# Weights of a two-block transformer split by DMAs instead of by the vector engines

## The chip, the cores and the metric

One core of one Trainium2 chip. The metric is device time in microseconds of one execution, the median of the runs. The core has a matrix engine (PE, with its weight loads as PEld), a vector engine (DVE), an activation engine (ACT), a general engine (POOL), and a queue that only issues transfers (SP). 16 DMA engines move data between main memory (HBM) and the on-chip memory (SBUF). Matrix products accumulate in PSUM.

## The reference, cut to what matters

x is 512 rows of 1024. The first block is attention of two kinds (differential, and sparse with compressed, selected and window branches), the second is a short convolution, top-k attention with an indexer, and a gated feed-forward:

```python
x = x + concat([o_diff, o_nsa]) @ w_out                       # first block
h = rms_norm(x, g_mix)                                        # second block
c_b, c_c, c_x, q, k, v, iq, ik, iw, g_a, g_b = split(h @ w_in_2)
y_a = short_conv(c_b, c_c, c_x) @ w_branch_a
y_b = dsa_attention(q, k, v, iq, ik, iw, rel_bias) @ w_branch_b
gates = sigmoid(concat([g_a, g_b]) + b_gate)
x = x + (gates[:, :1024] * y_a + gates[:, 1024:] * y_b) @ w_out_2
h2 = rms_norm(x, g_ffn)
x = x + (silu(h2 @ w_ffn_gate) * (h2 @ w_ffn_up)) @ w_ffn_down
return rms_norm(x, g_final)
```

All of it is float32. PE multiplies in a rounded form of it (float32r), so every operand is split into a high part (rounded) and a low part (what the rounding left), and one product is three matmuls: high by high, high by low, low by high (mm3).

## The kernel before, in words

A *unit* is one piece of a weight matrix, 128 partitions by nk by n. `K.unit` lists the units in the order in which they will be used; `_load` (L190) loads the next one into a tile "raw" on SP's queue, `_split` (L198) makes "whi" by a cast on ACT (L203) and "wlo" by a subtraction raw - whi (L205) on POOL or on DVE (the table POOL by phase: every third unit on POOL, every second, every one, or none), and `take` (L214) hands out the next split unit, splits one unit more and loads two beyond that.

The generators gen_ii, gen_i and gen_tt make the dense products from units, in short steps; the attention code runs such steps between its heads (`K.fill`), so that PE has work while softmax runs on DVE, ACT and POOL. Products of attention that must wait are deferred by planned times (LAG, LAG1 = 12000 ns, LAG2). gen_tt takes all its units at once. The order of the second block is: idx0, idx1, bq0, bq1 (three units each, each from two ranges of columns), conv (12 units), ga (8), ya (4), gb (8), then, when attention is done, yb (4), wo2 (four of gen_ii, four of gen_tt), and 40 units of w_ffn_down (32 of 128 x 2 x 256 and, before and after them, four each; the last four go through gen_tt). The gate and up weights of the feed-forward go another way: class Pair (L1252) loads them on SP and splits sums and differences of them on ACT and DVE; the w_ffn_down units are taken in small steps between its products.

Tiles come from a few tags with a fixed number of buffers. Most units are tag "k4" with 13 buffers, which they share with Pair's tiles, the probabilities (PTa), the gains (gB) and others; the small w_ffn_down units are tag "k2" with 19. A tile waits until a buffer of its tag is free. Each engine executes its instructions in order. The framework sets that order when it builds the program, by priority and by a simulated timeline, so an instruction can stand ahead of its place in the source if its inputs and its buffer are there earlier. A DMA is an instruction in the queue of the engine that issues it, and what stands behind it waits with it.

POOL's other work in the second block: the rows of the relative bias (L509 to L519, with two DMAs), the bias sums "bm" (L1498) and the scaling of softmax "p" (L1527) in attention, the power in the norms (L376, L377), and sums of "mg" (L1194).

Of the kernel before, what the change touches and what calls it, by code (L numbers as in the profile page):

```python
# [9 lines left out]
F32 = mybir.dt.float32  # L10
F32R = mybir.dt.float32r
AF = mybir.ActivationFunctionType
OP = mybir.AluOpType
AX = mybir.AxisListType.X

P = 128
# [17 lines left out]
POOL = {"s": 3, "d": 0, "n": 1, "i": 2, "t": 3, "b": 1, "f": 1}  # L34
# [12 lines left out]
class Kernel:  # L47

    def __init__(self, tc, pool, psum, dram, h):
        self.tc = tc  # L50
        self.nc = tc.nc
        self.pool = pool
        self.psum = psum
        self.dram = dram
        self.h = h
        self.clock = 0.0
        self.pending = []
        self.tails = []
        self.serial = 0
        self.queue = []  # L60
        self.after = None
        self.busy = False
        self.done = set()
        self.units = []
        self.raws = {}
        self.parts = {}
        self.loaded = 0
        self.split = 0
        self.taken = 0
        self.phase = "s"  # L70
        self.credit = 0.0
        self.filling = False
# [7 lines left out]
    def ps(self, shape, dt=F32, name="ps"):  # L80
        return self.psum.tile(shape, dt, name=name, tag="ps", bufs=8)
# [98 lines left out]
    def tick(self):  # L180
        c, self.cost = getattr(self, "cost", 0.0), 0.0
        if self.filling and not self.busy:
            self.credit -= c
        self.spend(c)


    def unit(self, srcs, nk, n, cls="k4", ns=5160.0):
        self.units.append((srcs, nk, n, cls, ns))

    def _load(self):  # L190
        srcs, nk, n, cls, _ = self.units[self.loaded]
        raw = self.t(cls, [P, nk, n], F32, "raw")
        for c0, ap in srcs:
            self.nc.sync.dma_start(raw[:, :, c0:c0 + ap.shape[-1]], ap)
        self.raws[self.loaded] = raw
        self.loaded += 1

    def _split(self):  # L198
        _, nk, n, cls, _ = self.units[self.split]
        raw = self.raws.pop(self.split)  # L200
        hi = self.t(cls, [P, nk, n], F32R, "whi")
        lo = self.t(cls, [P, nk, n], F32R, "wlo")
        self.nc.scalar.copy(hi, raw)  # L203
        every = POOL[self.phase]
        (self.nc.gpsimd if every and self.split % every == 0 else self.nc.vector).tensor_tensor(  # L205
            lo, raw, hi.bitcast(F32), op=OP.subtract)
        self.parts[self.split] = (hi, lo)
        self.split += 1

# [19 lines left out]
def krows(w, k0, nk, c0, n):  # L229
    return w[k0 * P:(k0 + nk) * P, c0:c0 + n].rearrange("(k p) n -> p k n", p=P)  # L230
# [18 lines left out]
def build(tc, pool, psum, dram, h):  # L249
    nc = tc.nc  # L250
    K = Kernel(tc, pool, psum, dram, h)
# [34 lines left out]
    def gen_ii(tag, lhs, w, cols, n, parts, evac, packed=True, wr=None, beside=(), cls="k4", ns=5160.0):  # L286
        for k0, nk in parts:
            srcs, c = [], 0
            for c0, m in cols:
                srcs.append((c, krows(w, (wr or 0) + k0, nk, c0, m)))  # L290
                c += m
            K.unit(srcs, nk, n, cls, ns)
            for piece in beside:
                piece.load()

        per = 2 if packed else 1

        def gen():
            banks = None
            for pi, (k0, nk) in enumerate(parts):  # L300
                wh, wl = K.take()
                if banks is None:
                    banks = [ps([P, per, n], name="acc") for _ in range(NT // per)]
                last = pi == len(parts) - 1
                for tt in range(NT):
                    a, bank = tt % per, banks[tt // per]
                    for k in range(nk):
                        K.mm3(bank[:, a, :], lhs(k0 + k, tt), (wh[:, k, :], wl[:, k, :]),
                              pi == 0 and k == 0 and a == 0, last and k == nk - 1)
                    if last and a == per - 1:  # L310
                        evac(tt - a, per, bank)
                    tick()
                    yield
                for piece in beside:
                    piece.step()
                    yield

        K.dense(tag, gen())
# [218 lines left out]
    def pair_split(src, n):  # L537
        q = t(cls(n), [P, n, 2, 64], F32R, "qs")
        A.copy(q[:, :, 0, :], src)
        V.tensor_sub(q[:, :, 1, :], src, f32(q[:, :, 0, :]))  # L540
        return q

    def dup_split(kn, n):
        kh = t(cls(n), [P, n, 2, 64], F32R, "kh")
        kl = t(cls(n), [P, n, 2, 64], F32R, "kl")
        b = kn[:, :, None, :].to_broadcast([P, n, 2, 64])
        A.copy(kh, b)
        V.tensor_sub(kl, b, f32(kh))
        return kh, kl

    def heads_T(src, n, t0, put, wait, tag):
        def go():
            for a in range(n):
                for eng, dst, srcs in put(a):
                    pt = ps([P, len(srcs), P], F32R, name="pt")
                    for c, s in enumerate(srcs):
                        K.tr(pt[:, c, :], s.rearrange("p l d -> p (l d)"), identR)
                    copy(eng, dst[:, :, (t0 + a) * P:(t0 + a + 1) * P], f32(pt))
            tick()
        defer(wait, go, tag)  # L560
# [538 lines left out]
    for nm in ORDER.split():  # L1099
        nm, _, b = nm.partition(":")  # L1100
# [25 lines left out]
    def i_evac(u):  # L1126
        def evac(tt, n, bank):
            qs = pair_split(bank[:, 0, 0:256].rearrange("p (c d) -> p c d", d=64), 4)
            heads_T(None, 1, tt, lambda a: [(A, S["iQ%d" % u], [qs[:, c] for c in range(4)])], LAG["i"], "idx")
            if u == 0:  # L1130
                kh, kl = dup_split(bank[:, :, 256:320], 1)
                heads_T(None, 1, tt, lambda a: [(V, S["iK"], [kh[:, 0], kl[:, 0]])], LAG["i"], "idx")
            else:
                A.activation(iws[:, tt, :], bank[:, 0, 256:264], AF.Copy, scale=8 ** -0.5 * 64 ** -0.5)
        return evac
# [66 lines left out]
        return f  # L1202

    K.after = None
    gen_ii("idx0", h2l, w_in2, [(2176, 256), (2688, 64)], 320, thirds, i_evac(0), packed=False)
    gen_ii("idx1", h2l, w_in2, [(2432, 256), (2752, 8)], 264, thirds, i_evac(1), packed=False)
    gen_ii("bq0", h2l, w_in2, [(1536, 256), (2048, 64)], 320, thirds, bq_evac(0), packed=False)
# [27 lines left out]
    for f0, nf in chunks:  # L1235
# [3 lines left out]
        if f0 + nf < 22:  # L1239
            for c0 in range(0, D, 256):  # L1240
                gen_ii("dn%d_%d" % (f0, c0), lhs, wd, [(c0, 256)], 256, parts_of(nf, 2), add_X(c0), wr=f0,
                       cls="k2", ns=DNS)
# [335 lines left out]
def emit(tc, h, stage="all"):  # L1578
    with tc.tile_pool(name="sb", bufs=1) as pool, \
            tc.tile_pool(name="ps", bufs=1, space=bass.MemoryType.PSUM) as psum, \  # L1580
            tc.tile_pool(name="dr", bufs=1, space=bass.MemoryType.DRAM) as dram, \
            contextlib.nullcontext():
        build(tc, pool, psum, dram, h)
# [18 lines left out]
```

## Time and profile before

| | |
|---|---|
| runs | 1082.15, 1079.30, 1080.58 us; median 1080.58 |
| profiled execution | 1079.54 us, span 1077.8 us |
| granted clock of TensorE, mean | 0.987 |
| PE, PEld busy | 97%, 90% |
| DVE, ACT, POOL busy | 64%, 52%, 38% |
| HBM read, written | 100.50 MB, 6.84 MB |
| DMAs on SP's queue (q1), on POOL's (q0) | 103.21 MB, 2.65 MB |

Times are microseconds from the start of the span. Busy shares are over the span; a matmul's end is modelled. The time of an execution is a little longer than the span of its core. L205 means line 205 of the kernel before.

### The profile page before, as it was taken

How to read it: one execution, taken by the hardware profiler on the slowest of the kernel's cores; microseconds unless marked ns; L12 is line 12 of the kernel's file. 1: busy time of each engine (PE TensorE's matmuls, PEld its weight loads, DVE VectorE, ACT ScalarE, POOL GpSimd, SP SyncE). 2: the span in 40 equal slices, each digit the busy share in tenths (PEclk: the TensorE clock that was granted, in tenths of full speed). 3: DMA queues.
4: the chain of work that ended last, by engine and by line, in shares of the span. 5: the costliest groups of instructions: out<-in, count | busy, mean ns of one | idle time of the engine just before them, and what ended most of it. 6: DMA issues, size and time to landing. Idle time of an engine off the chain costs nothing. (4 is left out here: it accounts for less than half of the span.)

```text
span 1077.8 us, 18966 instructions
## 1 busy us (share of the span) xinstructions
PE 1049.9 (97%) x7254; PEld 971.9 (90%) x7254; DVE 693.2 (64%) x1464; ACT 560.1 (52%) x1156; POOL 409.2 (38%) x403
## 2 busy tenths in 40 slices
PE   7999999999899999999999999988999999999997
PEld 7899898899789999888888888878999999999995
DVE  5777467356984638999125646477986666567734
ACT  5466687657973445523325765254543444444433
POOL 4442376555465241202127976500111222122241
PEclk8999999999999999999999999988999999999999
DMA  6446321321214335333241334421433223333022
GB/s 195 130 111 171 65 60 40 98 60 43 77 40 147 119 93 184 94 95 108 85 117 40 89 117 150 154 78 54 142 109 99 64 75 117 117 118 118 32 88 78
DMA packets 125045, 107.06 MB, mean 99 GB/s; under 512 B 20305, under 2 KB 115986, under 8 KB 124954
## 3 DMA queue, kind: packets, MB, share of 16 engines
q1 hardware_dynamic: 123882, 103.21, 31.5%
q0 software_dynamic: 1072, 2.65, 0.6%
q8 instruction: 57, 0.93, 0.4%
q14 instruction: 34, 0.28, 0.1%
HBM read 100.50 MB, written 6.84 MB: 100 GB/s over the span
## 5 line engine op out<-in xcount | busy, mean ns | idle before, releaser
L205 POOL TENSOR_TENSOR wlo<-raw,whi 128x1024 fp32r<-128x1024 f32 (+4 forms) x100 | 218.6, 2190 | 442.3 <-ACT whi L203 340.6
L163 PE MATMUL acc<-hA,wh 128*128 128x256 f32 x1232 | 223.7, 282 | 0.0
L163 PE MATMUL acc<-hT,whi 128*128 128x512 f32 x608 | 192.1, 395 | 0.2 <-ACT whi L203 0.2
L203 ACT CAST whi<-raw 128x1024 fp32r<-128x1024 f32 (+4 forms) x143 | 132.1, 925 | 115.7 <-PE acc L163 74.7
L163 PEld LDWEIGHTS acc<-hA,wh 128*128 128x128 f32 x1232 | 190.5, 190 | 0.1
L163 PE MATMUL acc<-whi,hT 128*128 128x256 f32 (+3 forms) x896 | 180.8, 291 | 0.5 <-ACT whi L203 0.5
L163 PE MATMUL acc<-hA,wl 128*128 128x256 f32 x616 | 173.1, 281 | 0.2 <-DVE wl L1249 0.2
L163 PEld LDWEIGHTS acc<-whi,hT 128*128 128x128 f32 x896 | 145.3, 191 | 1.3 <-ACT whi L203 0.7
L163 PEld LDWEIGHTS acc<-hT,whi 128*128 128x128 f32 x608 | 112.2, 188 | 23.5 <-ACT whi L203 0.4
L163 PE MATMUL acc<-whi,act 128*128 128x256 f32 (+1 forms) x640 | 132.8, 292 | 0.0
L163 PE MATMUL acc<-wlo,hT 128*128 128x256 f32 (+3 forms) x448 | 129.8, 290 | 0.7 <-POOL wlo L205 0.7
L163 PE MATMUL acc<-hT,wlo 128*128 128x512 f32 x304 | 120.5, 396 | 0.0
L163 PEld LDWEIGHTS acc<-hA,wl 128*128 128x128 f32 x616 | 116.7, 190 | 0.5 <-DVE wl L1249 0.4
L163 PEld LDWEIGHTS acc<-whi,act 128*128 128x128 f32 x640 | 105.0, 188 | 2.9
L1249 DVE TENSOR_TENSOR wl<-raw,wh 128x1024 fp32r<-128x1024 f32 x55 | 67.8, 1235 | 45.7 <-PE acc L163 24.9
L163 PE MATMUL acc<-wlo,act 128*128 128x256 f32 (+1 forms) x320 | 93.7, 293 | 0.0
L1248 ACT CAST wh<-raw 128x1024 fp32r<-128x1024 f32 x55 | 57.9, 1052 | 60.1 <-PE acc L163 41.8
L617 ACT ACTIVATE p<-p,s 128x128 f32<-128x128 f32 (+3 forms) x128 | 72.1, 565 | 31.5 <-DVE s L615 28.3
L163 PEld LDWEIGHTS acc<-wlo,hT 128*128 128x128 f32 x448 | 85.2, 190 | 1.4 <-POOL wlo L205 1.0
L205 DVE TENSOR_TENSOR wlo<-raw,whi 128x1024 fp32r<-128x1024 f32 (+5 forms) x43 | 52.8, 1231 | 41.1 <-ACT whi L203 41.0
L163 PEld LDWEIGHTS acc<-hT,wlo 128*128 128x128 f32 x304 | 57.2, 188 | 11.6
L163 PEld LDWEIGHTS acc<-wlo,act 128*128 128x128 f32 x320 | 60.2, 188 | 1.4
(271 smaller groups left out, 2011.7 us busy)
## 6 DMA issues: line engine op xcount, KB each, us to landing
raw<-in_w_in SPq DMA_DIRECT2D x52, 512.0 KB, 3.6
raw<-in_w_ffn_gate SPq DMA_DIRECT2D x22, 512.0 KB, 4.9
raw<-in_w_ffn_up SPq DMA_DIRECT2D x22, 512.0 KB, 6.1
raw<-in_w_ffn_down SPq DMA_DIRECT2D x36, 256.0 KB, 6.3
raw<-in_w_out SPq DMA_DIRECT2D x16, 512.0 KB, 3.6
raw<-in_cmp_w SPq DMA_DIRECT2D x8, 512.0 KB, 3.4
raw<-in_w_in SPq DMA_DIRECT2D x10, 384.0 KB, 3.7
rel_all<-rel_rows POOLq DMA_DIRECT2D x1, 2560.0 KB, 17.2
```

The lines of the kernel that those rows point to most:

```text
L163: self.nc.tensor.matmul(out, lhsT, rhs, start=start, stop=stop, skip_group_check=True)
L203: self.nc.scalar.copy(hi, raw)
L205: (self.nc.gpsimd if every and self.split % every == 0 else self.nc.vector).tensor_tensor(lo, raw, hi.bitcast(F32), op=OP.subtract)
L617: S["exp"] = A.activation(p[:, :n], p[:, :n], AF.Exp, scale=-1.0, bias=nm, accum_out=z).ins
L1248: A.copy(hi, src)
L1249: eng.tensor_tensor(lo, src, f32(hi), op=OP.subtract)
```

## The change: who splits a weight unit

For units that are listed after `K.by_dma = True`, that is all units of the second block, the raw tile is gone. The load goes to the queue of POOL and writes float32r, so the DMA rounds and the loaded tile is the high part. ACT writes the negative of the high part into the low part's tile. A second DMA on POOL's queue then loads the same weights from HBM again and adds them to what stands in that tile, which leaves weight minus high part.

```diff
     def unit(self, srcs, nk, n, cls="k4", ns=5160.0):
-        self.units.append((srcs, nk, n, cls, ns))
+        self.units.append((srcs, nk, n, cls, ns, self.by_dma))
 
     def _load(self):
-        srcs, nk, n, cls, _ = self.units[self.loaded]
-        raw = self.t(cls, [P, nk, n], F32, "raw")
+        srcs, nk, n, cls, _, by_dma = self.units[self.loaded]
+        raw = self.t(cls, [P, nk, n], F32R if by_dma else F32, "whi" if by_dma else "raw")
         for c0, ap in srcs:
-            self.nc.sync.dma_start(raw[:, :, c0:c0 + ap.shape[-1]], ap)
+
+            (self.nc.gpsimd if by_dma else self.nc.sync).dma_start(raw[:, :, c0:c0 + ap.shape[-1]], ap)
...
     def _split(self):
-        _, nk, n, cls, _ = self.units[self.split]
+        srcs, nk, n, cls, _, by_dma = self.units[self.split]
         raw = self.raws.pop(self.split)
-        hi = self.t(cls, [P, nk, n], F32R, "whi")
-        lo = self.t(cls, [P, nk, n], F32R, "wlo")
-        self.nc.scalar.copy(hi, raw)
-        every = POOL[self.phase]
-        (self.nc.gpsimd if every and self.split % every == 0 else self.nc.vector).tensor_tensor(
-            lo, raw, hi.bitcast(F32), op=OP.subtract)
+        if by_dma:
+
+            hi, lo = raw, self.t(cls, [P, nk, n], F32R, "wlo")
+            self.nc.scalar.activation(lo, hi.bitcast(F32), AF.Copy, scale=-1.0)
+            for c0, ap in srcs:
+                self.nc.gpsimd.dma_start(lo[:, :, c0:c0 + ap.shape[-1]], ap, accum_op=OP.add)
+        else:
+            hi = self.t(cls, [P, nk, n], F32R, "whi")
+            lo = self.t(cls, [P, nk, n], F32R, "wlo")
+            self.nc.scalar.copy(hi, raw)
+            every = POOL[self.phase]
+            (self.nc.gpsimd if every and self.split % every == 0 else self.nc.vector).tensor_tensor(
+                lo, raw, hi.bitcast(F32), op=OP.subtract)
...
     K.after = None
+    K.by_dma = True
     gen_ii("idx0", h2l, w_in2, [(2176, 256), (2688, 64)], 320, thirds, i_evac(0), packed=False)
```

## Rows read from the trace of the kernel before

**Rows 1.** Busy time, share of the span and instructions, from the page.

```profile
PE 1049.9 (97%) x7254; PEld 971.9 (90%) x7254; DVE 693.2 (64%) x1464; ACT 560.1 (52%) x1156; POOL 409.2 (38%) x403
```

**Rows 2.** Chain of waits, a piece: start us, us, engine, line.

```profile
748.39 322.30 PE acc L163 x2638
```

**Rows 3.** What PE waited for: us in total, times, longest us.

```profile
PE pt L177 <- DVE xs L1360: 7.2, 2, 3.7
PE acc L163 <- POOL wlo L205: 0.7, 1, 0.7
```

**Rows 4.** Busy us by stage, granted clock, DMA share, GB/s.

```profile
360.00:434.00 74.00, 73.93 (x534) 72.09 (x533) 47.84 (x100) 38.02 (x82) 22.54 (x44) 1.00 0.45 134
434.00:567.00 133.00, 133.00 (x592) 109.26 (x592) 87.24 (x169) 44.79 (x61) 26.69 (x13) 1.00 0.34 99
567.00:640.00 73.00, 73.00 (x398) 62.46 (x397) 42.50 (x152) 49.30 (x135) 59.45 (x68) 1.00 0.24 73
640.00:700.00 60.00, 59.31 (x357) 52.33 (x356) 31.48 (x36) 25.62 (x41) 38.27 (x23) 1.00 0.48 158
700.00:760.00 60.00, 51.72 (x359) 49.13 (x358) 48.49 (x60) 31.61 (x48) 3.29 (x5) 0.89 0.23 75
760.00:1078.00 318.00, 310.68 (x2542) 305.97 (x2540) 204.34 (x227) 135.27 (x189) 74.37 (x47) 0.99 0.29 95
```

**Rows 5.** Groups by line, 376 to 1078 us: count, busy us, mean ns, idle before.

```profile
L205 POOL TENSOR_TENSOR wlo<-raw,whi 128x512 fp32r<-128x512 f32 (+3 forms) x71 | 148.7, 2099 | 409.9 <-ACT whi L203 318.9 <-DVE gu L1312 50.6 <-PE acc L163 37.8
L203 ACT CAST whi<-raw 128x1024 fp32r<-128x1024 f32 (+4 forms) x91 | 79.1, 870 | 94.8 <-PE acc L163 65.9 <-issue 12.9 <-POOL wlo L205 6.6
```

**Rows 6.** The same of 360 to 434 us, then of 567 to 640 us.

```profile
L205 POOL TENSOR_TENSOR wlo<-raw,whi 128x960 fp32r<-128x960 f32 (+4 forms) x7 | 14.6, 2092 | 43.8 <-ACT whi L203 37.0 <-PE acc L163 6.8
L205 POOL TENSOR_TENSOR wlo<-raw,whi 128x1024 fp32r<-128x1024 f32 x8 | 19.5, 2448 | 6.3 <-ACT whi L203 6.2
```

**Rows 7.** DMA view, 434 to 567 us: bytes; issues, KB each, us to landing.

```profile
DMA packets 22653, 13.12 MB, mean 99 GB/s; under 512 B 432, under 2 KB 22261, under 8 KB 22645
raw<-in_w_in SPq DMA_DIRECT2D x19, 512.0 KB, 3.6
```

**Rows 8.** Timeline, conv's casts and first matmuls: start us, us, what.

```profile
417.35 1.07 ACT L203 CAST whi<-raw 128x1024 fp32r<-128x1024 f32 x1
433.11 0.65 PE L163 MATMUL acc<-hT,whi 128*128 128x512 f32 x2
451.96 1.05 ACT L203 CAST whi<-raw 128x1024 fp32r<-128x1024 f32 x1 [2.70 <-PE acc L163]
468.48 1.06 ACT L203 CAST whi<-raw 128x1024 fp32r<-128x1024 f32 x1 [3.10 <-PE acc L163]
```

**Rows 9.** Timeline of POOL, 398 to 404 us: its two DMAs.

```profile
399.86 0.82 POOL L518 DMA_DIRECT2D rel_rows<-rel  x1
402.30 1.12 POOL L519 DMA_DIRECT2D rel_all<-rel_rows  x1 [1.61 <-DMA rel_rows<-rel]
```

**Rows 10.** DMA view: the same two, KB each, us from issue to landing.

```profile
rel_all<-rel_rows POOLq DMA_DIRECT2D x1, 2560.0 KB, 17.2
rel_rows<-rel POOLq DMA_DIRECT2D x1, 20.0 KB, 2.1
```

**Rows 11.** Busy us of the stage before the feed-forward, as rows 4.

```profile
638.00:688.00 50.00, 49.31 (x317) 44.37 (x316) 26.76 (x29) 23.76 (x33) 38.53 (x19) 1.00 0.50 163
```

**Rows 12.** Timelines of SP, POOL and PE around the last units of wo2.

```profile
672.75 4.11 SPq L194 DMA_DIRECT2D raw<-in_w_out  x2
675.64 11.64 POOL L205 TENSOR_TENSOR wlo<-raw,whi 128x1024 fp32r<-128x1024 f32 x5
685.61 0.40 PE L163 MATMUL acc<-wlo,mg 128*128 128x512 f32 x1
```

**Rows 13.** Timelines of SP and PE where the feed-forward begins.

```profile
708.79 0.92 SPq L1265 DMA_DIRECT2D raw<-in_w_ffn_gate  x2
716.21 1.12 PE L177 MATMUL pt<-identF,xs 128*128 128x128 f32 x4 [3.53 <-DVE xs L1360]
```

More of the change, by code (lines that the diff above doesn't have):

```diff
@@ L67, in __init__ @@
         self.loaded = 0
+        self.by_dma = False
         self.split = 0
```

## The prediction

> **What bounds the kernel now.** I read the busy shares first: PE is busy 97% of the span, DVE 64%, ACT 52%, POOL 38% [rows 1]. A busy PE can still be held up between its pieces, so the chain of waits comes next: its last long piece is one unbroken run of 2638 matmuls, 322.30 us [rows 2]. Then PE's waits: over the whole span PE waited 0.7 us for a low part (wlo) of a weight; its one large wait is 7.2 us in two pieces for DVE's xs, which are activations, not weights [rows 3]. Last the stages. From 360 us on, which is where second-block weights are split, PE idles 16.4 us of 718 (718 - 701.63, the sum of the stages' PE column): nearly all of it in 700 to 760 us (8.28 us, at a mean clock of 0.89) and at the end of the program (7.32 us) [rows 4]. So PE's own work bounds the kernel, and splits are hidden already. An edit that makes splitting cheaper has that 0.7 us to win directly; an edit that makes a split arrive late loses time at full price.
>
> **The change, part by part.** 96 second-block units (12 of idx and bq, 12 conv, 8 ga, 4 ya, 8 gb, 4 yb, 8 wo2, 40 of w_ffn_down) change their split. The gate and up weights of Pair don't.
>
> *Removed: 96 subtractions.* Most stand on POOL: 71 after 376 us, 2.10 us each, 148.7 us [rows 5]; the others are DVE's. PE waited 0.7 us in all for them [rows 3], so their removal is worth between 0 and 0.7 us. I take 0.7.
>
> *ACT:* one cast becomes one scaled copy of the same size; the casts take 0.87 us each [rows 5], and ACT is busy 44.79 of 133 us in the densest stage [rows 4]. I take 0; a copy half as long again would add 12 us to 133, still hidden.
>
> *POOL issues 216 DMAs* (12 units with two sources, so 4 each, and 84 units with 2). The trace has two DMAs issued by POOL: 0.82 us for 20 KB and 1.12 us for 2560 KB [rows 9]. From below 0.82, from above the 2.1 us in which the small one was issued and landed [rows 10]; I take 1.12, the nearer in size. Densest for POOL is idx and bq: 48 issues, 54 us, beside about 8 us of other work (22.54 less 14.6 of subtractions) in the 74 us from 360 to 434 [rows 4, 6]. In 567 to 640 us POOL is busy 59.45 of 73 us; 8 subtractions (19.5 us) go and 16 issues (18 us) come [rows 4, 6]. Both fit: 0. What queues behind a POOL issue that waits for ACT's copy or for a free buffer are the softmax scalings (L1527) and bias sums (L1498), and PE's transposes wait for those; they are deferred by 12 us in the code (LAG1), so a wait of a few us stays covered.
>
> *Latency of a low part.* It was cast plus subtraction, 1.05 + 2.4 us; it becomes copy, issue and landing. A plain 512 KB load takes 3.6 us from issue to landing [rows 7], the 2560 KB one on POOL's queue 17.2 us [rows 10]. So 1.05 + 3.6 = 4.7 us from below, 18.3 us from above. The cover is the lead. Conv's first cast is at 417.35 us, its first matmuls at 433.11 us, and by the cast at 451.96 us, the eighth of conv, three units are done (24 matmuls each, a cast every (468.48 - 451.96)/3 = 5.5 us): the eighth unit's split starts 4 units, 22 us, before PE needs it [rows 8]. The units are held by the 13 k4 buffers, three to a unit before and two after, so the lead does not shrink. 18.3 us fits into 22. I take 0 for latency.
>
> *Bytes on the 16 DMA engines.* This is the term that I think decides. From 434 to 567 us the DMA share is 0.34 of 133 us, 45.2 us, for 13.12 MB [rows 4, 7]: 45.2/13.12 x 0.524 = 1.8 us of all engines per 512 KB. No row shows a rounding load or an accumulating one. The rounding load moves the bytes of a plain one: I take 1.8 (bounds 1.8 and twice that). The accumulating load must read the weights, read what stands in SBUF and write: not below a plain load, 1.8; I put the upper end at four plain loads, 7.2, an estimate from this row; I take 2.5 loads, 4.5 us (two reads instead of one, and half a load for the return trip that the read of the target adds). Per unit then 6.3 us against PE's 5.5. The 24 dense units (conv, ga, ya) fall behind by 24 x 0.8 = 19 us, and the lead of 22 us swallows that: 0 here, with little to spare (a rounding load at 3.6 us would make it 62 - 22 = +40), and gb's 8 units, which share 73 us with attention, let it recover.
>
> The rule that bears on it stands in the Trainium skill, page Collectives: The Full Stack, "The bandwidth ceiling": a reducing DMA is slower not by its addition but by its two source reads, which halve the rate. No run here shows it. By it the low part would cost 3.6 us, and the sum would be +3 in place of +10.
>
> Where the lead is gone is wo2, before the feed-forward. Its last two weights are loaded at 672.75 us, the last five subtractions end at 687.28 us, and the matmuls that need them (512 columns wide) start at 685.61 us: just in time [rows 12]. The DMA engines are busy 0.50 of the 50 us from 638 to 688 [rows 11], 25 us; some 3 us of it are gate and up loads that may come later. Added are 8 accumulating loads: 8 x 4.5 = 36 us. 22 + 36 = 58 us of work must end within the 48 us to 686: **+10 us**. PE has no other work there (yb and wo2 follow in a fixed order). With the accumulating load at 1.8 us: 22 + 14 = 36, nothing; at 3.6: 51, +3; at 7.2: 80, +32.
>
> *Feed-forward:* the DMA share is 0.29 of 318 us [rows 4]; 32 units of 256 KB and 4 of 512 KB add 20 x 4.5 = 90 us to 92: 0.57 of the stage, hidden. The last four units of w_ffn_down are taken together; their low parts may come 0 to 3 us late. I take 1.
>
> Sum: -0.7 + 10 + 1 = +10.3 us on the profiled execution's 1079.54 us (its span and 1.7 us around it), 1089.8. The median of the runs, 1080.58, is 1.0 us above that execution, so the forecast is 1091 us.
>
> **Rivals.**
> *It fits (25%).* The accumulating load costs two plain loads or less, everything is hidden, and the time is 1078 to 1084 us. For it: the 0.34 share leaves two thirds of the engines free. Against: the tight spot before 686 us. By the rule of the Trainium skill above this is the case, with +3. Were the load not to round at all, the low parts would be zero, but the same DMAs would run, so that changes no time.
>
> *Faster (12%).* PE idles before 716.21 us for 3.53 us and once more, for 7.2 - 3.5 = 3.7 us, waiting for xs, and the mean clock of 700 to 760 us is 0.89 [rows 3, 4, 13]; the 8.28 us of idling and 0.11 x 60 = 6.6 us of clock are 14.9 us. Pair 1's gate weights are loaded only at 708.79 us [rows 13], so its first two products (24 matmuls of 310.68/2542 = 0.12 us, 2.9 us each) can't fill the gap. Without a separate raw tile a k4 buffer could come free sooner. From a load 3.5 us earlier on, one product fills the first gap: -3.5 us of idling and part of the clock, -8 in all, 1072 us; with both gaps 1066. Against: just then 8 tiles of wo2, 4 of Pair 0 and the gain make 13 in either kernel.
>
> *POOL becomes the bound (13%).* From (74 - 8)/48 = 1.4 us an issue, idx and bq are held up by POOL. At 2.1 us: 48 x 2.1 + 8 - 74 = +35, with the +10 above: 1126 us. Against: 1.12 us for the large DMA [rows 9].
>
> *The accumulating load is four plain ones or more (15%).* 9.0 us a unit: 24 x 3.5 - 22 = +62 in the dense stage and +32 before 686 us: 1175 us. For it: the software queue's only large DMA moved 2560 KB in 17.2 us, 3.4 us per 512 KB before any addition [rows 10].
>
> **Chances and range.** The forecast gets 35%, with a range of its own of 1084 to 1105. What this kernel can tell from no change is about 0.3%, 3.2 us. Slower: 35 + 13 + 15%, and 0 of the case that fits: 63%; same 25%; faster 12%. The range reaches from 1075 (most of "it fits", a part of "faster") to 1165, past POOL as the bound and short of the slow accumulation; about 16% is left outside.
>
> **What would show it.** Right: PE waits for wlo from a DMA at about 680 to 700 us, a dense stage without waits, a DMA share near 1 from 434 to 567 us (24 x 6.3 = 151 us of work, less what the lead did before), a POOL issue of 1.1 us. Wrong: a POOL issue above 1.5 us; PE waits spread over every dense unit; a low part landing more than 22 us after its issue; a gate load well before 708 us. If the 434 to 567 us stage keeps its 133 us and 638 to 700 us its 60, it fits and I am wrong by the 10 us.

## The result and the profile after

The changed kernel takes 1109.16 us (median of 4 runs, 1106.63 to 1112.66) against 1080.11 us for the kernel before on the same chip (4 runs): ratio 1.0271, 95% interval 1.0246 to 1.0296, slower by 29 us. The forecast was 1091 us: slower, but by 10.

Lines of the changed kernel: mm L164, loads L196, ACT's negative L206, the adding load L208, the old cast and subtraction L212 and L214, the power in the norms L385 and L386. The page's busy row, which answers to [rows 1]; POOL's DMA issues count in it:

```profile
PE 1056.9 (96%) x7254; PEld 975.2 (88%) x7254; DVE 657.7 (59%) x1442; ACT 559.8 (51%) x1156; POOL 474.2 (43%) x545
```

PE's waits (us in total, times, longest us), the rows that answer to [rows 3]; its row for xs stays as it was (7.3 us, before 7.2):

```profile
PE pt L178 <- DVE xn L387: 7.3, 4, 3.3
PE acc L164 <- DMA wlo<-in_w_in: 4.2, 3, 2.0
PE acc L164 <- DMA wlo<-in_w_branch_b: 3.5, 2, 2.5
PE acc L164 <- DVE mg L1206: 3.4, 1, 3.4
PE acc L164 <- ACT at L1522: 2.9, 1, 2.9
PE acc L164 <- ACT part L1317: 2.5, 1, 2.5
```

The same view of the kernel before has two of these:

```profile
PE pt L177 <- DVE xn L378: 3.2, 2, 2.1
PE acc L163 <- DVE mg L1197: 0.7, 1, 0.7
```

PE now waits 7.7 us for low parts of w_in (idx and conv) and of w_branch_b (yb). It waits longer, 8.8 us, for things that are no weights: at (the output of attention), mg (the gated sums that wo2 takes) and part (a partial sum of the feed-forward); and 4.1 us more than before for xn, the normalized rows. For a low part of wo2 (w_out) it waits neither here nor in the trace of any other run. Busy time by stage, in the order of [rows 4] (us, then PE, PEld, DVE, ACT and POOL, clock, DMA share, GB/s); each window begins and ends at the matmul at which its row of before does:

```profile
361.20:442.80 81.60, 76.98 (x534) 73.71 (x533) 40.39 (x108) 39.80 (x89) 57.96 (x86) 0.98 1.00 168
442.80:577.70 134.90, 133.35 (x592) 109.36 (x591) 66.56 (x139) 42.94 (x53) 59.73 (x51) 1.00 1.33 208
577.70:650.70 73.00, 73.00 (x398) 62.54 (x398) 41.46 (x152) 50.74 (x137) 60.44 (x78) 1.00 0.68 115
650.70:723.70 73.00, 63.13 (x357) 54.72 (x356) 27.10 (x29) 21.69 (x31) 26.26 (x27) 0.95 0.93 214
723.70:785.20 61.50, 51.49 (x358) 48.80 (x357) 52.48 (x67) 33.86 (x56) 5.98 (x11) 0.89 0.24 73
785.20:1106.40 321.20, 311.06 (x2542) 305.89 (x2540) 199.01 (x226) 135.29 (x189) 74.30 (x82) 1.00 0.56 129
```

Against the 74, 133, 73, 60, 60 and 318 us of [rows 4]: idx and bq 7.6 us longer, conv to ya 1.9, attention with gb 0, yb and wo2 13.0, then 1.5 and 3.2. The densest stage, where the engines move most (share 1.33 in place of 0.34; packets overlap, so it can pass 1), loses almost nothing; the loss stands where a run of units begins or ends.

The table does the same for all kernels. Every trace holds 7254 matmuls, so the k-th of one is set against the k-th of before; cuts are where before stands at 360, 433, 640, 700 and 760 us after its first matmul. Columns: what is lost up to 360, in idx and bq, conv to gb, yb and wo2, the start of the feed-forward, the rest, and in all (us, from the one profiled execution of each).

```
                          <360  idx,bq conv-gb yb,wo2  700-760  rest   all
after                      1.1    7.7    1.9   13.0     1.5    3.2   28.4
e1  idx and bq only        1.5    8.2    1.3    0.0    -4.7    0.0    6.3
e2  conv to gb only        1.3    3.8    0.1    0.0    -4.7   -0.1    0.3
e3  yb and wo2 only        0.8   -0.0    1.7   16.0    -4.7    0.0   13.8
e4  down only              1.2   -0.0    1.7    0.0    -1.0    4.9    6.8
e5  e3, X later            1.2   -0.0    1.7   10.9    -3.1    0.0   10.7
e6  e1, one source         1.0   12.5    1.5    0.0    -3.1   -0.0   12.0
e7  all, more lead         2.3    6.4    5.2   10.7    -0.5   -0.0   24.1
e8  all, no second load    2.4    0.3    0.4    4.1    -3.1   -0.0    4.0
e9  all, second not adding 1.2    3.3    0.1    9.5     2.2   -0.1   16.1
e10 all, half added        1.6    5.8    0.0    4.1    -4.7   -0.0    6.8
e12 yb only                1.9   -0.0    1.7    2.2    -0.1    0.0    5.7
e13 e1, s first            1.4    4.3    1.1    0.0    -2.0    0.0    4.8
e14 e3, negative on POOL  -0.1    0.0    0.0   13.4    -0.9    0.0   12.4
e15 wo2 only               0.3    0.0    1.7    6.0    -3.3    0.0    4.7
e16 mended, without wo2    1.9    3.6    9.5    1.1    -3.2    0.0   12.9
e17 e16, rel_all on SP     1.0    4.9    1.2    2.9    -1.5   -0.0    8.4
e18 whole change, mended   0.5    5.0    2.1    5.5     4.6   -0.1   17.6
```

How far to trust it: up to 360 us nothing differs and the column still runs from -0.1 to 2.4; from 700 to 760 us e1, e2 and e3 change nothing and gain 4.7, since the clock falls to half there at other moments (before: mean 0.89 in [rows 4]). So a stage is good to some 2 us, that one to 5, and verdicts go by the medians. The 1.7 us in conv to gb stand in kernels that change nothing there (e3, e4, e15), and a wait that falls on a cut can move 1 to 2 us from one column to the next.

### The profile page after: what moved, and what is told of

The parts are those of the page before. It is cut to its first block, busy times and chain, and to the rows that moved or that the text cites. A ratio compares the mean times of both kernels' runs of the same rounds, so it can differ in the third digit from the quotient of the medians.

```text
span 1106.4 us, 19129 instructions
## 1 busy us (share of the span) xinstructions
PE 1056.9 (96%) x7254; PEld 975.2 (88%) x7254; DVE 657.7 (59%) x1442; ACT 559.8 (51%) x1156; POOL 474.2 (43%) x545
## 5 line engine op out<-in xcount | busy, mean ns | idle before, releaser
L164 PE MATMUL acc<-hA,wh 128*128 128x256 f32 x1232 | 223.0, 281 | 2.5 <-ACT part L1317 2.5
L164 PE MATMUL acc<-hT,whi 128*128 128x512 f32 x608 | 193.0, 396 | 0.2 <-ACT whi L212 0.2
L164 PEld LDWEIGHTS acc<-hA,wh 128*128 128x128 f32 x1232 | 189.9, 189 | 2.8 <-ACT part L1317 2.7
L164 PE MATMUL acc<-whi,hT 128*128 128x256 f32 (+3 forms) x896 | 181.4, 292 | 1.7 <-ACT whi L212 0.8
L164 PE MATMUL acc<-hA,wl 128*128 128x256 f32 x616 | 172.6, 280 | 0.5 <-DVE wl L1259 0.5
L164 PEld LDWEIGHTS acc<-whi,hT 128*128 128x128 f32 x896 | 145.6, 191 | 3.3 <-ACT hT L403 1.3
L208 POOL DMA_DIRECT2D wlo<-in_w_ffn_down x40 | 46.9, 1183 | 228.4 <-ACT wlo L206 211.5
L206 ACT ACTIVATE wlo<-whi 128x1024 fp32r<-128x1024 f32 (+4 forms) x96 | 84.1, 879 | 105.8 <-issue 25.6
L164 PE MATMUL acc<-wlo,hT 128*128 128x256 f32 (+3 forms) x448 | 130.5, 292 | 3.3 <-DMA wlo<-in_w_in 2.6
L164 PE MATMUL acc<-whi,act 128*128 128x256 f32 (+1 forms) x640 | 133.0, 292 | 0.0
L164 PEld LDWEIGHTS acc<-hT,whi 128*128 128x128 f32 x608 | 112.4, 188 | 22.4 <-ACT whi L212 0.4
L164 PE MATMUL acc<-hT,wlo 128*128 128x512 f32 x304 | 119.7, 395 | 1.5 <-DMA wlo<-in_w_in 1.5
L164 PEld LDWEIGHTS acc<-hA,wl 128*128 128x128 f32 x616 | 116.2, 189 | 0.8 <-DVE wl L1259 0.7
L164 PEld LDWEIGHTS acc<-whi,act 128*128 128x128 f32 x640 | 104.9, 189 | 2.9
L208 POOL DMA_DIRECT2D wlo<-in_w_in x52 | 79.5, 1825 | 34.7 <-ACT wlo L206 33.5
L164 PE MATMUL acc<-wlo,act 128*128 128x256 f32 (+1 forms) x320 | 93.9, 293 | 0.3 <-DMA wlo<-in_w_ffn_down 0.3
L164 PEld LDWEIGHTS acc<-wlo,hT 128*128 128x128 f32 x448 | 85.7, 191 | 4.5 <-DMA wlo<-in_w_in 2.2
L196 POOL DMA_DIRECT2D whi<-in_w_in x52 | 59.3, 1314 | 48.1 <-PE acc L164 48.1
L214 POOL TENSOR_TENSOR wlo<-raw,whi 128x1024 fp32r<-128x1024 f32 (+1 forms) x26 | 62.9, 2420 | 26.9 <-ACT whi L212 21.8
```

The costliest lines, as they stand in the source:

```text
L164: self.nc.tensor.matmul(out, lhsT, rhs, start=start, stop=stop, skip_group_check=True)
L196: (self.nc.gpsimd if by_dma else self.nc.sync).dma_start(raw[:, :, c0:c0 + ap.shape[-1]], ap)
L206: self.nc.scalar.activation(lo, hi.bitcast(F32), AF.Copy, scale=-1.0)
L208: self.nc.gpsimd.dma_start(lo[:, :, c0:c0 + ap.shape[-1]], ap, accum_op=OP.add)
```

## The experiments

**Which stages lose (e1 to e4).** The flag is set for some units only:

```diff
+    K.by_dma = False                     # e1: ahead of conv; e2: ahead of yb; e3: ahead of the down weights
-    K.by_dma = True                      # e2 to e4: set ahead of conv, of yb, of the down weights instead
```

e1: 

> Only the 12 units of idx and bq are split by DMAs. Theory (the loss is local, in the stages whose units have no lead): the whole loss of the idx and bq stage of the changed kernel stands here, +8 us, 1088, and nothing after that stage. Rival (the loss comes from a backlog that the DMA engines carry from stage to stage): less than half of that here, under +4. Second rival (POOL's 48 issues of these 12 units are what holds the stage): also +8 us, not told apart by this run.

Measured 1087.54 us, ratio 1.0081 (1.0063 to 1.0099), +8.1; the stage itself +8.2.

e2: 

> Only the 32 units of conv, ga, ya and gb are split by DMAs. Theory (loss only where there is no lead): 0 to +2 us, 1080 to 1082. Rival (bytes: these stages move the most, 6.8 us of summed packet time a unit, and push their backlog into what follows): +5 us or more, with waits for low parts up to the attention.

Measured 1081.56 us, ratio 1.0020 (1.0011 to 1.0030), +2.1. A third of the units, the densest ones, are almost free. What they cost stands at the start of conv, which the table still counts to idx and bq (3.8): ACT stands at the copy of a high part that has not landed, and PE waits for the activation r behind it. ACT's row, then PE's:

```profile
434.41 1.06 ACT L206 ACTIVATE wlo<-whi 128x1024 fp32r<-128x1024 f32 x1 [3.82 <-DMA whi<-in_w_in]
```

```profile
436.01 0.99 PE L164 MATMUL sc<-bK,qk 128*128 128x512 f32 x2 [2.29 <-ACT r L1478]
```

Behind that wait the granted clock is 0.50 (1.2 GHz) from 436.3 to 439.7 us, which costs 1.7 us more.

e3: 

> Only the 12 units of yb and wo2 are split by DMAs. Theory (local): +17 us, 1097, as the two stages lost in the changed kernel (7.4 and 9.6 us). Rival (the prediction's bytes before 686 us, with nothing in yb): +10 us. Second rival (a backlog that gb leaves behind): under +9.

Measured 1094.59 us, ratio 1.0141 (1.0124 to 1.0158), +15.1.

e4: 

> Only the 40 units of the down weights are split by DMAs. Theory: 0 to +2 us, 1080 to 1082: only the last four low parts are late. If the four parts add up to +25 to +31 us over these four runs, the loss is local; if their sum falls short by 8 us or more, something is carried across stages.

Measured 1086.41 us, ratio 1.0057 (1.0042 to 1.0073), +7.0, more than any theory had: 4.9 us of it at the very end. The four together make 32.3 us against 29, a little over the 25 to 31 put down and not short of them: the loss is local, and nothing large is carried from stage to stage.

**What in idx and bq (e6, e13).** POOL's timeline in the changed kernel (start, length, engine, line, operation, idle before):

```profile
363.36 3.13 POOL L196 DMA_DIRECT2D whi<-in_w_in  x4 [2.84 <-PE acc L164]
366.49 5.13 POOL L208 DMA_DIRECT2D wlo<-in_w_in  x4
369.54 3.57 POOL L196 DMA_DIRECT2D whi<-in_w_in  x2
373.20 0.29 POOL L385 TENSOR_SCALAR s<-s 128x1 f32<-128x1 f32 x1
373.55 2.64 POOL L208 DMA_DIRECT2D wlo<-in_w_in  x2
375.14 2.62 POOL L196 DMA_DIRECT2D whi<-in_w_in  x2
376.71 3.71 POOL L208 DMA_DIRECT2D wlo<-in_w_in  x2
378.32 2.71 POOL L386 TENSOR_TENSOR s<-s,mhalf 128x1 f32<-128x1 f32 x1
```

POOL gets buffers at 363 us and then issues without a pause. The two tiny operations that finish a norm (s, L385 and L386) stand between the issues and end at 381.03 us. DVE's next row shows who waits, against an idle time of 0.85 us at 366.73 us before:

```profile
381.06 0.75 DVE L387 SCALAR_TENSOR_TENSOR xn<-X,s,gB 128x512 f32<-128x512 f32 x1 [10.46 <-POOL s L386]
```

e6 halves the issues:

```diff
-    gen_ii("idx0", h2l, w_in2, [(2176, 256), (2688, 64)], 320, ...      # idx1, bq0, bq1 alike
+    gen_ii("idx0", h2l, w_in2, [(2176, 320)], 320, ...
```

> As the run with idx and bq alone split by DMAs (+8 us), but each unit loads its columns from one place (320 or 264 neighbouring columns, so other weights of the same size): 24 DMAs from POOL in place of 48. Theory (POOL's issues, two to four in a row at 1.3 us and more, hold back the first low parts): +3 us or less. Rival (the hop from ACT's copy over the issue to the landing is too long for the first units whatever their count of DMAs): +6 to +8.

Measured 1091.47 us, ratio 1.0113 (1.0087 to 1.0140), +12.2: worse than either range, so as put down the theory fails. The trace splits it. Ten microseconds into the stage e6 had lost 2.6 us where e1 had lost 5.1, as expected of fewer issues. But at 434 us PE waits 7.2 us once, since rel_all (2560 KB) now came ahead of the last low part in POOL's queue. POOL's rows, then PE's:

```profile
414.70 1.17 POOL L528 DMA_DIRECT2D rel_all<-rel_rows  x1 [5.85 <-PE acc L164]
421.70 1.25 POOL L208 DMA_DIRECT2D wlo<-in_w_in  x1 [5.84 <-ACT wlo L206]
```

```profile
434.35 0.63 PE L164 MATMUL acc<-wlo,hT 128*128 128x320 f32 x1 [7.21 <-DMA wlo<-in_w_in]
```

The low part took 12.6 us from issue to use. rel_all landed 17.7 us after its issue, at 432.4. e13 keeps all issues and only puts s first:

```diff
-        G.tensor_tensor(r, r, mhalf, op=OP.pow)
+        K.s_last = G.tensor_tensor(r, r, mhalf, op=OP.pow).ins
...
+            with self.tc.issue_after(self.s_last):      # POOL's loads of later units, and all adding loads
```

> Only idx and bq split by DMAs (+8 us), but POOL issues their DMAs behind the normalization of the last rows (s), which in that run ended at 381 us in place of 367 because eight issues stood ahead of it. Theory (s is late, and with it xn, hT and the matmuls of the last rows): the loss falls to +2 to +4 us. Rival (the low parts are late whatever POOL does first; they are issued no earlier here): +6 to +8.

Measured 1083.14 us, ratio 1.0041 (1.0025 to 1.0056), +4.1: half of the loss was s. DVE now waits 1.84 us for it:

```profile
368.11 0.75 DVE L390 SCALAR_TENSOR_TENSOR xn<-X,s,gB 128x512 f32<-128x512 f32 x1 [1.84 <-POOL s L389]
```

The other half stays: PE still waits 1.85 us for a low part at 374 us.

**What a load costs by itself (e11).** No computation; sections of 8 x 512 KB, `dma_start(tile, weights)` from SP or POOL into float32 or float32r tiles, and with `accum_op=OP.add`; DVE reads one element of each tile as it lands.

> Leaves the whole computation out and only moves weights: sections of 8 loads of 512 KB each, in rows of 1 KB and then of 512 B: plain from SP, plain from POOL, rounding from POOL, accumulating from POOL onto a rounded and onto a plain tile; at the end 8 accumulating loads beside 2 x 1 MB from SP. The prediction's prices: 1.8 us a unit plain and rounding, 4.5 accumulating. From the packets of the changed kernel I expect a section of 8 to take 15 us plain, 20 us rounding and 35 us accumulating in 1 KB rows (1.8, 2.5 and 4.3 us a unit), more in 512 B rows, and an issue of 0.8 us rounding and 1.3 us accumulating in both.

DVE's rows, the idle time before each and the transfer that ended it: plain from POOL, rounding and adding in 512 B rows (bt, ct, dt), plain from SP and rounding in 1 KB rows (aw, cw), and adding in 1 KB rows (dw), an early row and a later one:

```profile
149.81 0.15 DVE L64 COPY mark<-bt_pool 128x1 f32<-128x1 f32 x1 [1.65 <-DMA bt_pool<-in_w_ffn_gate]
160.63 0.15 DVE L64 COPY mark<-ct_round 128x1 f32<-128x1 f32 x1 [1.64 <-DMA ct_round<-in_w_ffn_gate]
190.19 0.15 DVE L64 COPY mark<-dt_add 128x1 f32<-128x1 f32 x1 [2.72 <-DMA dt_add<-in_w_ffn_gate]
18.29 0.15 DVE L64 COPY mark<-aw_sp 128x1 f32<-128x1 f32 x1 [1.36 <-DMA aw_sp<-in_w_ffn_gate]
56.42 0.15 DVE L64 COPY mark<-cw_round 128x1 f32<-128x1 f32 x1 [1.33 <-DMA cw_round<-in_w_ffn_gate]
68.48 0.15 DVE L64 COPY mark<-dw_add 128x1 f32<-128x1 f32 x1 [2.42 <-DMA dw_add<-in_w_ffn_gate]
83.06 0.15 DVE L64 COPY mark<-dw_add 128x1 f32<-128x1 f32 x1 [3.65 <-DMA dw_add<-in_w_ffn_gate]
```

From one landing to the next (idle time and copy), 512 KB takes 1.8 us plain, 1.8 rounding and 2.9 adding in 512 B rows; in 1 KB rows it takes 1.5 us plain and rounding. The adding section in 1 KB rows did not run alone: from 67.17 us SP loaded the tiles of the next sections beside it. The queues from 72 to 91 us (packets, MB, share of the engines):

```profile
q0 software_dynamic: 2410, 2.39, 78.6%
q1 hardware_dynamic: 3466, 1.75, 40.4%
```

So the 3.8 us of the later row is what an adding load takes beside 1.75 MB of plain loads for 2.39 MB of its own kind. The earlier row, most of it ahead of these loads, gives 2.6 us. The changed kernel agrees: two low parts of yb (1 KB rows), issued at 647.62 and 648.85 us, land 16.3 and 17.8 us later, 2.7 us apart, after X has landed. I take 2.6. Against what was put down for 1 KB rows (1.8, 2.5 and 4.3), rounding and adding are both much cheaper.

What POOL spends on issuing (length of 1, 1, 8 and 8 issues):

```profile
41.76 0.74 POOL L79 DMA_DIRECT2D cw_round<-in_w_ffn_gate  x1 [1.19 <-DVE mark L64]
148.70 0.87 POOL L79 DMA_DIRECT2D ct_round<-in_w_ffn_gate  x1 [1.13 <-DVE mark L64]
59.88 10.37 POOL L81 DMA_DIRECT2D dw_add<-in_w_ffn_gate  x8 [15.12 <-DVE mark L64]
168.23 12.51 POOL L81 DMA_DIRECT2D dt_add<-in_w_ffn_gate  x8 [13.29 <-DVE mark L64]
```

An issue is 0.74 or 0.87 us for a rounding load (1 KB, then 512 B rows), 1.30 or 1.56 for an adding one. The last section says nothing: its 2 x 1 MB from SP ran at 20 us, beside other sections.

**What in yb and wo2 (e5, e12, e15, e14).** Here SP, no longer held by weights that wait for buffers, issues X (2 x 1 MB) at 646.97 us; before it was 666.09 us. The changed kernel is 10.7 us behind when it issues X, so by PE's progress X comes some 30 us earlier. What ACT does meanwhile in the changed kernel, and then in the kernel before:

```profile
660.88 1.06 ACT L206 ACTIVATE wlo<-whi 128x1024 fp32r<-128x1024 f32 x1 [9.39 <-DMA whi<-in_w_out]
668.22 1.06 ACT L206 ACTIVATE wlo<-whi 128x1024 fp32r<-128x1024 f32 x1 [6.28 <-DMA whi<-in_w_out]
670.63 0.62 ACT L1522 CAST at<-ob 128x512 fp32r<-128x512 f32 x1 [0.75 <-DVE ob L664]
672.57 5.02 ACT L1572 ACTIVATE sg<-sg,vec 128x512 f32<-128x512 f32 x8
```

```profile
648.98 0.62 ACT L1512 CAST at<-ob 128x512 fp32r<-128x512 f32 x1 [0.75 <-DVE ob L655]
650.91 5.02 ACT L1562 ACTIVATE sg<-sg,vec 128x512 f32<-128x512 f32 x8
```

ACT stands at two copies until high parts of wo2 land. The last copy of attention (at) stands behind them, and behind that, by the order that the code sets, the sigmoids sg, without which there is no mg; they start 21.7 us later than before. PE's waits in the two stages are 3.5 us for two low parts of yb, 2.9 for at and 3.4 for mg (0.7 before); as the wait for mg ends, the granted clock is 0.50 from 683.7 to 690.5 us, another 3.4 us. That is 12.5 of the 13.0 us. The transfers issued from 640 to 653 us (count, KB each, median us to landing):

```profile
wlo<-in_w_branch_b POOLq DMA_DIRECT2D x4, 512.0 KB, 14.0
X<-x1d SPq DMA_DIRECT2D x2, 1024.0 KB, 11.2
whi<-in_w_out POOLq DMA_DIRECT2D x3, 512.0 KB, 17.7
whi<-in_w_branch_b POOLq DMA_DIRECT2D x2, 512.0 KB, 4.4
```

By e11's prices that is 4 x 2.6 + 2 x 1.5 + 3 x 1.5 + 4 x 1.5 = 23.9 us of work. It is issued from 640.0 to 651.8 us, and the last of it, a high part of wo2, lands 17.7 us after its issue, at 669.5: the high parts for which ACT stands have low parts of yb ahead of them in POOL's queue and X beside them. e5 lets ACT issue X behind the first mg of yb:

```diff
-            MAKE["X"] = lambda: X_load(x1d)
+            MAKE["X"] = X_late      # with tc.issue_after(S["mg0"]): X_load(x1d, nc.scalar); mg0: first copy of mg
```

> As the run with yb and wo2 alone split by DMAs (+15 us), but the two loads of X (2 x 1 MB) are issued by ACT behind the first mg copy of yb, about where they stood before the change (666 us), so that they no longer run beside the low parts of yb and the high parts of wo2. Theory (SP's queue, freed of the weights, starts X 24 us early, and that collision is what the two stages lose): +3 to +6 us, 1083 to 1086. Rival (the prediction's: the bytes of 8 accumulating loads before 686 us are too many for the engines): still +10 or more, since the bytes are the same.

Measured 1090.24 us, ratio 1.0099 (1.0074 to 1.0125), +10.9 against +15.1: in the rival's range and not in the theory's. X is over a quarter of the loss, not the most. Without it, the high part at which ACT stands last is issued at 644.79 us and still lands 12.3 us later: three low parts of yb and a high part are ahead of it in POOL's queue, 3 x 2.6 + 1.5 us, and its own 1.5 makes 10.8.

e12 and e15 set the flag for one of the two only, as in e1 to e4.

e12: 

> Only the 4 units of yb are split by DMAs; wo2's weights stay on SP's queue, so X is loaded as late as before the change and no high part of wo2 stands behind a low part of yb. Theory (the loss in yb and wo2 is the queue: high parts of wo2 behind low parts of yb, beside an early X, with ACT stuck at the copies): 0 to +3 us. Rival (the low parts of yb are late by themselves): +5 or more.

Measured 1082.24 us, ratio 1.0013 (0.9994 to 1.0031), no change clear of the noise; the stage +2.2.

e15: 

> Only the 8 units of wo2 split by DMAs; yb as before, so no low part of yb stands ahead of wo2's high parts on POOL's queue. Theory (queue order): 0 to +4 us, so that with yb alone (+2) the two make far less than the +15 of both together. Rival (the prediction's bytes: 8 accumulating loads in wo2): +8 to +12, as the prediction had it.

Measured 1085.03 us, ratio 1.0056 (1.0034 to 1.0077), +6.0, the stage +6.0: between the two ranges. PE waits for no low part here. ACT's rows, then PE's:

```profile
651.74 1.06 ACT L206 ACTIVATE wlo<-whi 128x1024 fp32r<-128x1024 f32 x1 [8.05 <-DMA whi<-in_w_out]
656.19 5.02 ACT L1573 ACTIVATE sg<-sg,vec 128x512 f32<-128x512 f32 x8
```

```profile
668.26 0.50 PE L164 MATMUL acc<-whi,mg 128*128 128x256 f32 x2 [2.87 <-DVE mg L1206]
```

ACT stands 8.05 us at a high part that came beside X (issued at 641.67 us in this run), the sigmoids start 5.3 us later than before, and PE waits for mg. The granted clock is 0.50 from 669.1 to 675.9 us, behind that wait: 3.4 us of the 6.0. yb alone and wo2 alone make 8.2 us, together 16.0: with both, wo2's high parts stand behind yb's low parts. e14 takes the copy off ACT:

```diff
-            self.nc.scalar.activation(lo, hi.bitcast(F32), AF.Copy, scale=-1.0)
+            self.nc.gpsimd.tensor_scalar(lo, hi.bitcast(F32), -1.0, 1.0, op0=OP.mult, op1=OP.mult)
```

> Only yb and wo2 split by DMAs (+15 us), but the negative of the high part is made by POOL in place of ACT, so that ACT no longer stands at a high part that hasn't landed. Theory (ACT's stop of 14.8 us before the last attention copies is most of the loss): +5 to +9 us; ACT's wait for whi of w_out gone, PE's 4.4 us wait for at gone. Rival (the bytes in front of 686 us): +13 to +16.

Measured 1094.26 us, ratio 1.0148 (1.0120 to 1.0176), +15.2: nothing gained. ACT's stops and PE's wait for at are gone, but POOL stops at the same transfer (8.26 us), and POOL issues the adding loads and forms the sums mg: PE waits 5.2 us for low parts of yb (2.7 in e3) and 3.4 for mg. POOL's row, then PE's:

```profile
653.43 1.05 POOL L206 TENSOR_SCALAR wlo<-whi 128x1024 fp32r<-128x1024 f32 x1 [8.26 <-DMA whi<-in_w_out]
```

```profile
658.00 0.50 PE L164 MATMUL acc<-at,wlo 128*128 128x512 f32 x1 [3.21 <-DMA wlo<-in_w_branch_b]
```

So my theory that freeing ACT wins falls: the stop moves to the engine that makes the copy, and what stands behind it there is late in its place. No run here leaves both engines free, so it isn't shown how much late transfers cost when nothing stands behind them.

**How much of it is the addition (e8, e9, e10).** Only the second load is changed: left out, made to overwrite, or halved.

```diff
-                self.nc.gpsimd.dma_start(lo[:, :, c0:c0 + ap.shape[-1]], ap, accum_op=OP.add)      # e8
+                self.nc.gpsimd.dma_start(lo[:, :, c0:c0 + ap.shape[-1]], ap)                       # e9
+                self.nc.gpsimd.dma_start(lo[:, :(nk + 1) // 2, c0:c0 + w], ap[:, :(nk + 1) // 2, :w], accum_op=OP.add)  # e10
```

e8: 

> The whole change without the accumulating loads: the low part stays the negative of the high part (wrong values, same instructions else). What remains is the rounding loads on POOL's queue, 108 issues, and SP's queue without weights. Theory (late low parts at idx and at the end; X beside wo2's high parts): idx 0 to +2, yb and wo2 +6 to +10 from X and the high parts alone, end 0: 1086 to 1092. Rival (all of the loss comes from the accumulation): within 3 us of before.

Measured 1083.04 us, ratio 1.0035 (1.0023 to 1.0048), +3.7: less than I gave it, and just over the rival's 3. X is early there too (639.30 us); beside it the high parts alone cost 4.1 us in yb and wo2 by the table, all of what this run loses.

e9: 

> The whole change, but the second load of each part overwrites the low part with the rounded weights instead of adding to it (wrong values; the same DMAs, waits, issues and bytes read from HBM, but no read of the target). Theory A (what costs is the hop: a second DMA whose issue waits for ACT's copy and which lands some us later): most of the loss stays, 1102 to 1108. Theory B (what costs is the longer packets of an accumulating load, about 65 ns against 42 ns for 512 B): half or more of the loss goes, 1090 to 1096.

Measured 1094.96 us, ratio 1.0128 (1.0098 to 1.0157). That is in theory B's range, with a little under half of the loss gone. e8 leaves 3.7 us, a second load adds 12, the addition 14 more: each theory has about half. In idx the loss falls from 7.7 to 3.3 us; four issues of the second load take 2.95 us in place of 5.13, and s ends at 376.6 us instead of 381.

e10: 

> The whole change, but each accumulating load adds only half of the low part's rows (for the last wo2 weights half the columns; the rest stays the negative of the high part): the same count of DMAs from POOL and the same waits, half the packets. Theory A (hop): the idx stage loses its 7 us all the same, 1100 to 1106. Theory B (packets): half of the loss or more goes, 1090 to 1096, most of it in yb and wo2.

Measured 1096.71 us, ratio 1.0134 (1.0088 to 1.0181), just over theory B's range, but its runs go from 1087.89 to 1098.60 and the profiled one is the fastest. Idx loses 5.8 us of the 7.7 with half the bytes, as POOL's issues would have it; the rest of its row is no evidence.

**The lead, and the mending together (e7, e16, e17, e18).** e7 splits two units ahead:

```diff
-                self.split <= j or sum(u[4] for u in self.units[j + 1:self.split]) < SPLITS):
+                self.split <= j or sum(u[4] for u in self.units[j + 1:self.split]) < (8000 if self.units[j][5] else SPLITS)):
```

> The whole change, but a split may run two units ahead of its use instead of one (8 us of estimated matmul time in place of 3). Theory (what is lost at the start of idx, in yb and at the end is the missing lead): the idx stage loses 3 us instead of 7.5, the end 1 instead of 3.3, yb and wo2 keep their loss since X still collides: 1100. Rival (bytes or POOL's issues): as the change, 1109.

Measured 1104.43 us, ratio 1.0235 (1.0213 to 1.0256), 4 us over what the theory had. The end is mended (3.2 to 0.0), idx hardly (7.7 to 6.4): its first units have nothing in front of them to be ahead of. Conv to gb gets worse (1.9 to 5.2). At the end of the changed kernel, ACT stands at the copy of a down weight, and part, for which PE waits, is behind it; these are its rows:

```profile
1065.49 1.06 ACT L206 ACTIVATE wlo<-whi 128x1024 fp32r<-128x1024 f32 x1 [4.62 <-DMA whi<-in_w_ffn_down]
1066.45 0.57 ACT L1317 COPY part<-acc 128x512 f32<-128x512 f32 x1
```

With more lead, part goes ahead of that copy. e16 is e7 with s first (as in e13) and wo2 split as before:

> The whole change except wo2 (split as before), with s ahead of the DMA issues and splits up to two units ahead (8 us). If the causes named are all there is: idx +2 to +4, conv to gb 0 to +2, yb +2, the end 0: 1083 to 1087, two thirds of the loss gone. If something else costs, such as POOL's issues in all stages or the bytes: above 1093.

Measured 1089.97 us, ratio 1.0094 (1.0069 to 1.0120), 3 us over the upper end. 6.7 us of it go at the start of conv, where PE waits 3.58 us for a low part issued right behind rel_all, with the granted clock at half for 6.8 us around it. e17 is e16 with that transfer on SP:

```diff
-        G.dma_start(rel_all, rel_rows[:, None, :].to_broadcast([8, P, 640]))
+        nc.sync.dma_start(rel_all, rel_rows[:, None, :].to_broadcast([8, P, 640]))
```

> As the run with the causes mended and wo2 left out (1090), but rel_all (2560 KB) is issued by SP, not by POOL. Theory (the first low parts of conv stand behind it in POOL's queue): the 6.7 us at the start of conv fall to 0 to 2, 1083 to 1086. Rival (too many bytes for the engines there, whichever queue): still 5 us or more, 1088 to 1092.

Measured 1087.43 us, ratio 1.0057 (1.0037 to 1.0076), 1.4 us over the theory's range: the 6.7 us became 0.5, the bytes being the same, so it was the place in the queue. e18 is e17 with wo2 by DMA again and X later:

> The whole change, wo2 too, with s first, splits up to two units ahead, rel_all on SP's queue and X loaded as late as before the change. Theory: idx +4, conv 0 to 2, the end 0, and in yb and wo2 what the engines can't move in time, 12 low parts at 3.8 us and their high parts: +8 to +11 there; together 1091 to 1097. Rival (the loss in yb and wo2 was only the backlog of what stood before, or the early X): under 1087.

Measured 1094.61 us, ratio 1.0131 (1.0110 to 1.0152): in the range expected, and half of the loss is gone. The total is right in part by luck: yb and wo2 lose 5.5 us, not the 8 to 11 that 3.8 us an adding load gave, and the profiled execution, the slowest of four, has 4.6 us more in the stage that is good to 5. No version beats the kernel before.

## Why the prediction was wrong

It forecast +10 us, all but a microsecond of it in one place and by one mechanism: the bytes of wo2's eight adding loads. The kernel lost 29, in several places, and PE never waits for a low part of wo2.

*Right:* PE's own work bounds both kernels. Splits were hidden already, so the saved subtractions show nowhere. A unit by DMA costs next to nothing in the dense stage: conv to gb alone +2.1, at its start. The place of the largest loss, just before the feed-forward, was named; that +10 was forecast there and 13.0 lost is luck, as the next points show.

*Failed: "ACT: I take 0".* ACT's busy time is as forecast (559.8 us against 560.1), but busy time was all that was weighed. The copy that makes the low part needs a high part that comes by POOL's queue; until it lands ACT stands, and what is behind the copy in ACT's order is late: at, the sigmoids and with them mg, and part at the end. PE waits 2.9, 3.4 and 2.5 us for them, 8.1 more than before, and the clock that falls behind mg makes it 11.5 of the 29. e15 shows it with no late low part beside it (+6.0), e2 in small; e14 shows that the same copy on POOL is no better.

*Failed: "what queues behind a POOL issue".* The prediction named the softmax scalings and the bias sums, and called POOL's issues hidden because 54 us fit into 74. The sum was nearly right: 46 issues in 360 to 435 us take 27.8 + 36.0 = 63.8 us, 1.39 each. But they come in a burst, and the norm's two operations on POOL, a row of the code that the prediction passed over, stood in it. That is 4 of the 8 us of idx (e13). The rest goes to low parts that are late.

*Failed: "the cover is the lead".* 22 us of lead were measured in conv [rows 8] and taken for all units. The first units of a run have none: in idx POOL gets its buffers at 363.36 us and PE wants the low parts from 369 on. At the end the lead was one unit; two made the 3.2 us vanish (e7).

*Mis-sized: the adding load.* 4.5 us was the price; 2.9 (512 B rows) and 2.6 (1 KB rows) are measured. At 1.8 + 2.9 = 4.7 us a unit the dense stage keeps up with PE's 5.5 without using the lead. The Trainium skill, Collectives: The Full Stack, "The bandwidth ceiling", has the reducing transfers of a collective at half the rate of copies for their two reads; measured here are ratios of 2.9/1.8 = 1.6 and 2.6/1.5 = 1.7, so an adding load is somewhat cheaper than that rule has it.

*Failed: "58 us in 48".* With the measured price (the 1 KB one for all eight loads) the account gives 22 + 8 x 2.6 = 43 in 48, which fits, and the forecast would have been no loss at all. What it left out are yb's four adding loads, behind which wo2's high parts queue, and X, which SP brings forward once weights no longer hold its queue: 23.9 us of transfers issued within 12 us from 640 on, so that high parts of wo2 land 15 to 18 us after their issue. The prediction looked at what was moved to POOL's queue and not at what moved up in SP's.

*A cost nobody forecast:* low parts behind rel_all in POOL's queue: a wait of 7.2 us in e6, 3.6 in e16, and by its place, though not tried there, the 1.55 us at 452.87 us in the changed kernel. The Trainium skill, DMA: Bandwidth & Descriptors, "SWDGE vs HWDGE vs iDMA", has one context for all of the transfers that POOL issues; e6 and e17 agree with it.

*The rivals.* "It fits" had the price right (two plain loads or less; measured 1.6 to 1.7) and drew the wrong conclusion from it: cheap transfers were not hidden, because of their order. "Four plain loads or more" is out by e11. "Faster" did not come: Pair 1's gate load is issued at 736.37 us, 27.6 us later than before, which is how late PE is by then. "POOL becomes the bound from 1.4 us an issue" was nearer than its 13%: the mean was 1.39.

*Open.* How much of the 13 us of yb and wo2 would stay if no engine stood at a high part: e14 moves the stop from ACT to POOL, and e8 to e10 change the order of the program with the bytes. And 1.5 us of the loss from 700 to 760 us can't be told from that stage's own scatter.

## What to carry to other kernels

Moving work from compute engines to DMAs moves waits into queues: list, for each queue that gains or loses instructions, the small operations behind the new ones and the transfers that can now start earlier. Count transfers against the window between the moment buffers come free and the first use, at the start and the end of each run of units and not over a stage. Keep what a critical engine needs out of the order behind a copy that waits for a load, on whichever engine that copy is. And when you time a transfer by itself, see in the trace that nothing else ran beside it.

## What the hardware showed unexpectedly

An adding load costs 1.6 to 1.7 plain ones: 2.9 us per 512 KB against 1.8 in rows of 512 B, 2.6 against 1.5 in rows of 1 KB; beside plain loads of another queue it took 3.8. A rounding load costs what a plain one does. An adding load of 512 KB in such rows takes POOL 1.30 to 1.56 us to issue, nearly twice a rounding one.
